# Two-layer encoder on one core: where the memory keys are transposed, how the memory values are split, and when some sums are made in the first chunks

## The chip, the core and the metric

One NeuronCore of a Trainium2 chip runs the whole kernel as one program. The metric is the device time of one execution in microseconds (us); the median of several runs counts. In the profiled execution the granted clock of TensorE was 1.00 throughout.

## The reference, cut to what matters

Two encoder layers on 512 tokens of width 1024, all in float32. Layer 0 mixes tokens with dilated window attention, layer 1 with grouped-query attention; both also attend, with 4 heads of 128, into 256 memory tokens:

```python
def memory_attention(q_mem, mem_h, w_kv, qn_g, kn_g):
    q = rmsnorm(q_mem.reshape(Bn, S, MEM_HEADS, HEAD_DIM), qn_g) * (HEAD_DIM ** -0.5)
    kv = jnp.einsum('bnd,de->bne', mem_h, w_kv).reshape(Bn, N, 2, MEM_HEADS, HEAD_DIM)
    k = rmsnorm(kv[:, :, 0], kn_g)
    v = kv[:, :, 1]
    s = jnp.einsum('bqhe,bkhe->bhqk', q, k).astype(jnp.float32)
    p = jax.nn.softmax(s, axis=-1).astype(v.dtype)
    return jnp.einsum('bhqk,bkhe->bqhe', p, v).reshape(Bn, S, MEM_W)
```

Each layer norms its input, projects it with one wide weight matrix, gates the heads' outputs and projects back: `x = x + jnp.einsum('bse,ed->bsd', y, w_out[i])`. The change concerns the first stretch of layer 0: the memory keys and values, and the first projections of x.

## The kernel before, in words

**Precision by halves.** Every float32 factor is split into a rounded part and a remainder. ScalarE (ACT) casts a weight tile to `wh` (L313), VectorE (DVE) subtracts to get `wo` (L323), and TensorE (PE) multiplies activation high by weight high (L175), activation low by weight high (L176) and activation high by weight low (L179). Four `wh` and four `wo` buffers form a ring.

**Seven products.** A projection of x is made by a scheme with seven products of half-size quarters instead of eight (`s_chunk`). The activations' combinations are called 12, 11, S1, S2, S4, S3, 22 in the order of the products; the weights' are "21", "11", T1, T2, "22", T3, T4. T1 is made by a DVE addition of two loaded pieces (L282), T2 by a DMA issued from GpSimd (POOL) that adds T1 onto another piece (L287), T3 by such a DMA from the weights in DRAM (L292), T4 by one that adds T2 onto "21" (L297). Bank by bank, ACT keeps a snapshot `sn` of a product (L388) and DVE adds the next ones to it (L405, L399). S2 and S4 come from DVE sums (L577, L579) behind S1 and S3 (L565, L566); each combination is then split by an ACT cast (L163, L573) and a DVE subtraction (L166, L574).

**What sets the order.** The program of each engine is written out in a fixed order while a `Driver` counts slots. After each group of matmuls on PE (a group: one pair of weight tiles on one block, or one weight tile on all blocks) the driver's `tick` advances a slot and resumes the generators that are due: `yield n` in one of them means "go on n slots later". `drv.release` starts one after a bank is complete, `drv.late` and `drv.soon` put a function at the end of this slot or the start of the next. `Weights.advance` runs once per group: it splits at most two weight tiles, makes at most one weight sum (`sum`), casts up to two tiles (`hi`) and issues loads (`dma`). `ripe` says how many groups must have passed since a load was issued or a sum made: LEAD = 2 unless told otherwise.

**The first chunks**, in the order in which PE takes them: the memory keys (four groups), the memory values (four groups), then the first projection by seven products (14 groups of 2.72 us: the values of the first window group, `v0`), then the memory queries (7 groups), then the eight heads. In between, PE transposes: x into `xT` for the activations (`turn4`, L505), and the normed memory keys into `qT` (`transpose4`, L610). Both use the four PSUM buffers of tag `at`. A group's result stands in one of four buffers `pj`.

**The memory keys and values** (`mem_kv`). A block of 128 keys is normed (L598, L453, L603), transposed two slots later (L610), and written as `kmT` by ACT (L647) and, LO_K[0] = 9 slots later, its remainder by DVE (L650). A block of values is scaled by ACT from PSUM to `vm` (L675) and its remainder made by DVE from the same PSUM bank (L678) at once, so the bank is held until DVE has read it. `kmT` and `vm` are read by the memory attention, whose first scores stand behind the first head's third product.

**Buffers.** 23 SBUF buffers of tag `m4` (128 x 1024) hold weight pieces, x, the key and value tiles and more. A load takes a free one when the program is written, and waits on the chip for the last reader of what was in it.

Of the kernel before, what the change touches and what calls it, by code (L numbers as in the profile page):

```python
# [10 lines left out]
F32 = mybir.dt.float32  # L11
F32R = mybir.dt.float32r
AF = mybir.ActivationFunctionType
ALU = mybir.AluOpType
# [11 lines left out]
MEM_STEP = 1, 1  # L26
MEM_D = 4
DIRECT, DIRECT_B = (7,), (4, 5, 6, 7)
LO_K, LO_V = (9, 5), (0, 3)
PD = 2  # L30
EO = 2, 2, 1, 2, 2, 1
YB = {"m": (2, 2), "k": (1, 1, 1), 0: (1, 2, 1), 1: (1, 2, 1)}
# [10 lines left out]
KEEP_C = {0: 14, 3: 14, 4: 12}  # L43
# [87 lines left out]
def trunk_kernel(ctx: ExitStack, tc: tile.TileContext, x, mem, wall, norm_g, mem_norm_g, gcol,  # L131
                 qn_a, kn_a, qn_b, kn_b, ident_d, mask_d, tab_a, tab_b, out):
    nc = tc.nc
    V, A, G, T = nc.vector, nc.scalar, nc.gpsimd, nc.tensor
# [11 lines left out]
    def m4(dt=F32, name="m4"):  # L146
        return pool.tile([128, 1024], dt, tag="m4", name=name, bufs=NM4)
# [47 lines left out]
    class Weights:  # L195
# [71 lines left out]
        def sum(self, force=False, want=None):  # L267

            for n, (key, d) in enumerate(self.sums[:8]):
                if want and key != want:  # L270
                    continue
                c, k, x = key
                if not c and not force and self.g < SUM_AT.get(k, 0):
                    break
                if k == "T1" and c >= T1_DMA:
                    if not self.ripe(self.load_at, key, force):
                        continue
                    G.dma_start(self.tile[key], wall[d], accum_op=ALU.add)
                elif k == "T1":
                    if not (self.ripe(self.load_at, key, force) and self.ripe(self.at, (c, "11", x), force)):  # L280
                        continue
                    V.tensor_tensor(self.tile[key], self.tile[key], self.tile[c, "11", x], ALU.add)  # L282
                    self.use((c, "11", x))
                elif k == "T2":
                    if not (self.ripe(self.load_at, key, force) and self.ripe(self.at, (c, "T1", x), force, 1 if c < T1_DMA else None)):
                        continue
                    G.dma_start(self.tile[key], self.tile[c, "T1", x], accum_op=ALU.add)  # L287
                    self.use((c, "T1", x))
                elif k == "T3":
                    if not self.ripe(self.load_at, key, force):  # L290
                        continue
                    G.dma_start(self.tile[key], wall[d], accum_op=ALU.add)  # L292
                else:
                    if not (self.ripe(self.lo_at, (c, "21", x), force, 1) and self.ripe(self.at, (c, "T2", x), force, T4_AT.get(c))):
                        continue
                    self.tile[key] = self.tile[c, "21", x]
                    G.dma_start(self.tile[key], self.tile[c, "T2", x], accum_op=ALU.add)  # L297
                    self.use((c, "T2", x))
                self.at[key] = self.g
                self.sums.pop(n)  # L300
                return True
            return False
# [161 lines left out]
    rm = pool.tile([128, 6], F32, name="rm")  # L464
# [188 lines left out]
    def mem_kv(layer, M, mid=None):  # L653
        kt_ = [m4(F32R, "kmT").rearrange("p (h t) -> p h t", h=4) for _ in range(2)]
        vt_ = [m4(F32R, "vm").rearrange("p (b e) -> p b e", b=2) for _ in range(2)]

        def ev_k(b, p):
            r = head_sq(p) if layer else head_sq(p, by=rm[:, 2 + b:3 + b])

            def rest():  # L660
                if not layer:
                    G.tensor_scalar(r, r, rm[:, b:b + 1], None, ALU.mult)
                xn = head_mul(p, r)
                yield 2
                q = transpose4(xn)
                cs = slice(b * 128, (b + 1) * 128)
                yield from put_norm(q, gk_m[layer], kt_[0][:, :, cs], kt_[1][:, :, cs], LO_K[layer])

            drv.release(rest(), 2)
            yield 1  # L670

        def ev_v(b, p):

            h = 0.5 if layer else rm[:, 4 + b:5 + b]
            A.activation(vt_[0][:, b], p, AF.Copy, scale=h)  # L675
            if b and LO_V[layer]:
                yield LO_V[layer]
            V.scalar_tensor_tensor(vt_[1][:, b], p, h, vt_[0][:, b].bitcast(F32), ALU.mult, ALU.subtract)  # L678
            yield 1

        proj_t(M, NAT[:2], ev_k, mid)
        proj_t(M, NAT[:2], ev_v)
        return kt_, vt_

# [276 lines left out]
    def prep():  # L961

        n = {}
        for c in range(5):
            if c < 4:
                n[c] = norm_1(xb[c], c == 2)
            if c:
                norm_2(xb[c - 1], n[c - 1], rows["x"])
            if 1 < c < 4:
                first_t(H, xb[c - 2], c - 2)  # L970
            yield 1

        def forms(c):
            yield from diffs_t(H, xb[2 + c], c)
            yield 2
            yield from rest_t(H, c, (2, 2, 2))

        drv.spawn(forms(1), 1)
        yield from forms(0)
# [57 lines left out]
    p = turn4(mg[0, 0], None, None)  # L1037
# [631 lines left out]
```

## Time and profile before

| What | Value |
|---|---|
| Median of 3 runs | 953.63 us (952.09 to 953.82) |
| The profiled execution | 953.29 us, its span 951.4 us |
| PE busy | 937.2 us of the span (99%) |
| VectorE (DVE) busy | 790.0 us (83%) |
| ScalarE (ACT) busy | 681.1 us (72%) |
| GpSimd (POOL) busy | 340.0 us (36%) |
| PE's idle time in the first 100 us that it spent waiting for DVE | 3.6 us in three waits (2.3, 0.9, 0.4) |

A row of a timeline gives start, duration, engine, line of the kernel, operation, output<-input, shape and count, and in brackets how long the engine had been idle before and what ended that. Rows of instructions that follow each other on one engine overlap a little (one DVE operation of 128 x 1024 shows 1.22 us, and the next starts 1.13 us after it), so distances are taken from start to start. The 1.9 us between the span and the time of the profiled execution lie around the span and belong to every run.

### The profile page before, as it was taken

How to read it: one execution, taken by the hardware profiler on the slowest of the kernel's cores; microseconds unless marked ns; L12 is line 12 of the kernel's file. 1: busy time of each engine (PE TensorE's matmuls, PEld its weight loads, DVE VectorE, ACT ScalarE, POOL GpSimd, SP SyncE). 2: the span in 40 equal slices, each digit the busy share in tenths (PEclk: the TensorE clock that was granted, in tenths of full speed). 3: DMA queues.
4: the chain of work that ended last, by engine and by line, in shares of the span. 5: the costliest groups of instructions: out<-in, count | busy, mean ns of one | idle time of the engine just before them, and what ended most of it. 6: DMA issues, size and time to landing. Idle time of an engine off the chain costs nothing.

```text
span 951.4 us, 16573 instructions
## 1 busy us (share of the span) xinstructions
PE 937.2 (99%) x5680; PEld 830.7 (87%) x5680; DVE 790.0 (83%) x1411; ACT 681.1 (72%) x1698; POOL 340.0 (36%) x484
## 2 busy tenths in 40 slices
PE   8999999999999999999999999999899999999998
PEld 6789888888888888888889998888899999998886
DVE  6997676878888888889798999868978998769982
ACT  7775689676868686868676768457778886878860
POOL 3323323656554545464827011213233241011110
PEclk9999999999999999999999999999999999999999
DMA  9999946869787878696868989979876686776524
GB/s 352 387 252 326 283 97 160 298 118 273 153 254 148 258 154 265 156 266 133 254 169 194 275 202 247 283 275 297 227 166 140 179 237 174 213 201 177 127 57 127
DMA packets 86198, 203.51 MB, mean 214 GB/s; under 512 B 25057, under 2 KB 34529, under 8 KB 86114
## 3 DMA queue, kind: packets, MB, share of 16 engines
q1 hardware_dynamic: 66962, 139.46, 42.9%
q0 software_dynamic: 17856, 60.83, 34.3%
q10 hardware_dynamic: 1296, 2.16, 0.6%
q8 instruction: 45, 0.74, 0.3%
q14 instruction: 39, 0.32, 0.1%
HBM read 156.48 MB, written 11.34 MB: 176 GB/s over the span
## 4 chain that ended last, share of the span: by engine, by line
PE 90%; DVE 4%; ACT 2%; DMA 2%; issue 1%; POOL 0%; SPq 0%; DVEq 0%; ACTq 0%; POOLq 0%
PE pj L176 24%; PE pj L175 24%; PE pj L179 24%; PE qT L610 2%; PE sa L1189 2%; PE oo L1297 2%; PE pt L1276 1%; PE ptb L1499 1%; DVE wo L323 1%; PE sa L1185 1%; PE ob L179 1%; DMA odb<-o 1%; PE pmt L735 1%; DMA m<-in_mem_dram 1%; PE ob L176 1%
## 5 line engine op out<-in xcount | busy, mean ns | idle before, releaser
L323 DVE TENSOR_TENSOR wo<-wl,wh 128x1024 fp32r<-128x1024 f32 x255 | 315.0, 1241 | 6.3 <-ACT wh L313 5.9
L313 ACT CAST wh<-wl 128x1024 fp32r<-128x1024 f32 x255 | 268.8, 1060 | 32.9 <-PE pj L176 19.2
L175 PE MATMUL pj<-wh,hS 128*128 128x512 f32 (+1 forms) x448 | 157.4, 365 | 1.7 <-DVE sn L405 1.7
L176 PE MATMUL pj<-wh,hS 128*128 128x512 f32 (+1 forms) x448 | 152.2, 353 | 0.6 <-DVE hS L574 0.6
L175 PE MATMUL pj<-wh,h 128*128 128x512 f32 (+1 forms) x336 | 117.8, 364 | 0.0
L176 PE MATMUL pj<-wh,h 128*128 128x512 f32 (+1 forms) x336 | 114.1, 353 | 1.1 <-DVE h L574 1.1
L453 POOL TENSOR_TENSOR rstd<-mse,half 128x4 f32<-128x4 f32 (+2 forms) x96 | 101.4, 1056 | 8.0
L179 PE MATMUL pj<-wo,hS 128*128 128x512 f32 (+1 forms) x448 | 99.9, 352 | 0.0
L175 PEld LDWEIGHTS pj<-wh,hS 128*128 128x128 f32 x448 | 84.8, 189 | 12.1 <-DVE sn L405 2.1
L176 PEld LDWEIGHTS pj<-wh,hS 128*128 128x128 f32 x448 | 84.9, 190 | 11.0 <-DVE hS L574 0.8
L179 PEld LDWEIGHTS pj<-wo,hS 128*128 128x128 f32 x448 | 74.7, 189 | 11.8
L452 POOL TENSOR_SCALAR mse<-hss 128x4 f32<-128x4 f32 (+1 forms) x86 | 42.6, 495 | 112.9 <-ACT junk L598 108.5
L388 ACT COPY sn<-pj 128x512 f32<-128x512 f32 x116 | 64.5, 590 | 24.0 <-PE pj L179 23.2
L1133 POOL TENSOR_TENSOR ta<-sn,tabs 128x128 f32<-128x128 f32 (+1 forms) x64 | 39.8, 629 | 116.6 <-DVE sn L603 91.1
L598 ACT ACTIVATE junk<-sn 128x128 f32<-128x128 f32 x264 | 79.2, 309 | 1.2 <-DVE sn L399 1.2
L179 PE MATMUL pj<-wo,h 128*128 128x512 f32 (+1 forms) x336 | 74.8, 352 | 0.0
L176 PEld LDWEIGHTS pj<-wh,h 128*128 128x128 f32 x336 | 63.7, 190 | 8.8 <-DVE h L574 1.3
L175 PEld LDWEIGHTS pj<-wh,h 128*128 128x128 f32 x336 | 63.6, 189 | 7.3
L405 DVE TENSOR_TENSOR sn<-pj,sn 128x512 f32<-128x512 f32 x87 | 59.6, 686 | 8.5 <-PE pj L179 8.1
L297 POOL DMA_DIRECT2D wl<-wl x33 | 29.5, 903 | 103.7 <-DVE wo L323 54.5
L179 PEld LDWEIGHTS pj<-wo,h 128*128 128x128 f32 x336 | 56.0, 189 | 8.8
L287 POOL DMA_DIRECT2D wl<-wl x33 | 31.3, 976 | 72.7 <-DVE wl L282 21.4
(252 smaller groups left out, 2363.6 us busy)
## 6 DMA issues: line engine op xcount, KB each, us to landing
wl<-in_wall_dram SPq DMA_DIRECT2D x222, 512.0 KB, 7.4
wl<-wl POOLq DMA_DIRECT2D x66, 512.0 KB, 6.2
wl<-in_wall_dram POOLq DMA_DIRECT2D x42, 512.0 KB, 8.6
od<-o SPq DMA_DIRECT2D x11, 256.0 KB, 5.7
og<-od SPq DMA_DIRECT2D x10, 256.0 KB, 9.4
x<-in_x_dram SPq DMA_DIRECT2D x4, 512.0 KB, 9.0
v0d<-sn SPq DMA_DIRECT2D x8, 256.0 KB, 8.4
acc<-in_x_dram POOLq DMA_DIRECT2D x8, 256.0 KB, 6.4
```

What stands on the lines that cost most here:

```text
L175: T.matmul(o, a, b, start=start, stop=False, skip_group_check=True)
L176: T.matmul(o, c, d, start=False, stop=False, skip_group_check=True)
L179: T.matmul(o, a, b, start=False, stop=stop, skip_group_check=True)
L287: G.dma_start(self.tile[key], self.tile[c, "T1", x], accum_op=ALU.add)
L313: A.copy(wh, self.tile[self.items[i]])
L323: V.tensor_tensor(wo, self.tile[key], wh.bitcast(F32), ALU.subtract)
L388: A.copy(t, b)
L405: V.tensor_tensor(t, b, t, ALU.subtract if q == "12" else ALU.add)
L452: G.tensor_scalar(e, ss, EPS, None, ALU.add)
L453: G.tensor_tensor(r, e, half[:, 0:n], ALU.pow)
L598: A.activation(jk, p[:, j * 128:(j + 1) * 128], AF.Square, scale=by, accum_out=ss[:, j:j + 1])
L1133: G.tensor_tensor(ta[:, 0:n], xn[:, 0:n, 0:32], ropeA[:, 0, b, s0:s0 + n], ALU.mult)
```

## The change

Four edits; all act on layer 0's first chunks alone (for layer 1 the old numbers and the old way of making the values stay).

- **Keys transposed later.** The wait ahead of the transposes `qT` goes from 2 to 8 slots (`TURN_K[0]`), and that of the remainder behind them from 9 to 4 (`LO_K[0]`).
- **Values split from a copy.** ACT first copies the scaled bank to a new SBUF tile `vr` (L682), one slot later casts it to `vm` (L684), and DVE makes the remainder nine slots after that from `vr` and `vm`, both in SBUF (L686). There is one more `m4` buffer in use, and two more ACT instructions.
- **S2 and S4 later.** `forms` waits 3 slots instead of 2 before the sums for the fourth and fifth product.
- **T1 later.** For the chunks named in KEEP_C (the first projection, the memory queries and the first head) the DVE addition for T1 must wait four groups after its load is issued instead of two.

```diff
-LO_K, LO_V = (9, 5), (0, 3)
+LO_K, TURN_K, LO_V = (4, 5), (8, 2), (9, 3)
...
-                    if not (self.ripe(self.load_at, key, force) and self.ripe(self.at, (c, "11", x), force)):
+                    if not (self.ripe(self.load_at, key, force, 4 if c in KEEP_C else None) and self.ripe(self.at, (c, "11", x), force)):
...
+        raw = None if layer else m4(name="vr")
...
-                yield 2
+                yield TURN_K[layer]
...
-            h = 0.5 if layer else rm[:, 4 + b:5 + b]
-            A.activation(vt_[0][:, b], p, AF.Copy, scale=h)
-            if b and LO_V[layer]:
+            if layer:
+                A.activation(vt_[0][:, b], p, AF.Copy, scale=0.5)
+                if b:
+                    yield LO_V[layer]
+                V.scalar_tensor_tensor(vt_[1][:, b], p, 0.5, vt_[0][:, b].bitcast(F32), ALU.mult, ALU.subtract)
+            else:
+                t = raw[:, b * 512:b * 512 + 512]
+                A.activation(t, p, AF.Copy, scale=rm[:, 4 + b:5 + b])
+                yield 1
+                A.copy(vt_[0][:, b], t)
                 yield LO_V[layer]
-            V.scalar_tensor_tensor(vt_[1][:, b], p, h, vt_[0][:, b].bitcast(F32), ALU.mult, ALU.subtract)
+                V.tensor_tensor(vt_[1][:, b], t, vt_[0][:, b].bitcast(F32), ALU.subtract)
...
         def forms(c):
             yield from diffs_t(H, xb[2 + c], c)
-            yield 2
+            yield 3
             yield from rest_t(H, c, (2, 2, 2))
```

Up to the memory values, and from the first head on, each engine's instructions stand in the same order as before; the line numbers behind the edits are higher by 8. In between, three places matter. The first is VectorE's program from the second half of the normed x (L499) to the S1 of both token halves (`hS`), before:

```order
L499 SCALAR_TENSOR_TENSOR x<-x,rstd,row 128x512 x2
L323 TENSOR_TENSOR wo<-wl,wh 128x1024 x2
L678 SCALAR_TENSOR_TENSOR vm<-pj,rm,vm 128x512
L282 TENSOR_TENSOR wl<-wl 128x1024
L565 TENSOR_TENSOR fS_515<-xT,f_476 128x512
L566 TENSOR_TENSOR fS_516<-f_369,xT 128x512
L166 TENSOR_TENSOR hS_519<-fS_515,hS_519 128x4x128
L678 SCALAR_TENSOR_TENSOR vm<-pj,rm,vm 128x512
```

and with the change:

```order
L499 SCALAR_TENSOR_TENSOR x<-x,rstd,row 128x512 x2
L323 TENSOR_TENSOR wo<-wl,wh 128x1024 x2
L282 TENSOR_TENSOR wl<-wl 128x1024
L565 TENSOR_TENSOR fS_509<-xT,f_477 128x512
L566 TENSOR_TENSOR fS_510<-f_370,xT 128x512
L166 TENSOR_TENSOR hS_513<-fS_509,hS_513 128x4x128
L323 TENSOR_TENSOR wo<-wl,wh 128x1024 x2
```

Both remainders of the values have left this place; they stand some 30 instructions later. On PE, the transposes `xT` and `qT` ahead of the first projection's first groups (`h` is the split x), before, where a line of dots stands for the L175 and L176 rows of a group:

```order
L505 MATMUL xT<-ident,x 128x128 x8
L610 MATMUL qT<-ident,xn 128x128 x4
...
L179 MATMUL pj<-wo,act 128x512 x4
L610 MATMUL qT<-ident,xn 128x128 x4
L505 MATMUL xT<-ident,x 128x128 x8
...
L179 MATMUL pj<-wo,h_351 128x512 x4
```

and with the change, where the two `qT` stand behind the fifth and sixth group of the projection (S1, `hS`):

```order
L505 MATMUL xT<-ident,x 128x128 x8
...
L179 MATMUL pj<-wo,act 128x512 x4
L505 MATMUL xT<-ident,x 128x128 x8
...
L179 MATMUL pj<-wo,hS_513 128x512 x4
L610 MATMUL qT<-ident,xn 128x128 x4
...
L179 MATMUL pj<-wo,hS_513 128x512 x4
L610 MATMUL qT<-ident,xn 128x128 x4
```

PE has two transposes fewer ahead of the first projection, and two `at` buffers fewer are taken there. The third place is VectorE again, from the setup of the rotary tables (`grA`) to the snapshots of the memory queries, before:

```order
L992 TENSOR_SCALAR grA<-grA 128x96
L405 TENSOR_TENSOR sn<-pj,sn 128x512
L323 TENSOR_TENSOR wo<-wl,wh 128x1024 x2
L282 TENSOR_TENSOR wl<-wl 128x1024
L323 TENSOR_TENSOR wo<-wl,wh 128x1024
L399 TENSOR_TENSOR sn<-sn 128x512 x2
L405 TENSOR_TENSOR sn<-pj,sn 128x512
L323 TENSOR_TENSOR wo<-wl,wh 128x1024
L282 TENSOR_TENSOR wl<-wl 128x1024
```

and with the change:

```order
L1000 TENSOR_SCALAR grA<-grA 128x96
L686 TENSOR_TENSOR vm<-vr,vm 128x512
L405 TENSOR_TENSOR sn<-pj,sn 128x512
L323 TENSOR_TENSOR wo<-wl,wh 128x1024 x3
L399 TENSOR_TENSOR sn<-sn 128x512 x2
L405 TENSOR_TENSOR sn<-pj,sn 128x512
L323 TENSOR_TENSOR wo<-wl,wh 128x1024
L282 TENSOR_TENSOR wl<-wl 128x1024
```

The first of the two T1 additions of the first head (L282) now stands behind a third split, the two L399 and an L405, and one of the values' remainders stands right behind the setup. On ACT, the two casts L684 stand around the cast of the first T1 tile, and the casts of the first T2 tile and of S2's second half have changed places.

## The prediction

> **What bounds the kernel now.** I read the page first, then PE's waits in the first 100 us, then the timelines of PE, DVE, ACT and POOL around the two larger waits. The page:
>
> ```profile
> span 951.4 us, 16573 instructions
> PE 937.2 (99%) x5680; PEld 830.7 (87%) x5680; DVE 790.0 (83%) x1411; ACT 681.1 (72%) x1698; POOL 340.0 (36%) x484
> ```
>
> PE is the bound, so only a gap on PE is worth time, and an instruction moved along PE's program is worth none. PE's waits on DVE in the stretch that the change touches (us in total, times, longest):
>
> ```profile
> PE xT L505 <- DVE fS L566: 2.3, 1, 2.3
> PE pj L175 <- DVE sn L405: 0.9, 1, 0.9
> ```
>
> **The first gap, from PE's timeline:**
>
> ```profile
> 31.43 1.07 PE L179 MATMUL pj<-wo,act 128*128 128x512 f32 x4
> 32.35 1.03 PE L505 MATMUL xT<-ident,x 128*128 128x128 f32 x8
> 33.22 0.60 PE L610 MATMUL qT<-ident,xn 128*128 128x128 f32 x4
> 33.57 0.48 PE L175 MATMUL pj<-wh,act 128*128 128x512 f32 x1
> 35.51 1.08 PE L179 MATMUL pj<-wo,act 128*128 128x512 f32 x4
> 36.43 0.60 PE L610 MATMUL qT<-ident,xn 128*128 128x128 f32 x4
> 36.87 0.60 PE L505 MATMUL xT<-ident,x 128*128 128x128 f32 x4
> 39.78 0.63 PE L505 MATMUL xT<-ident,x 128*128 128x128 f32 x4 [2.32 <-DVE fS L566]
> 42.08 1.07 PE L179 MATMUL pj<-wo,h 128*128 128x512 f32 x4
> ```
>
> Between the L179 of 31.43 and that of 35.51 lie eight xT, four qT and one group: 4.08 us. From there to 42.08 the same work took 6.57, so the gap costs 6.57 - 4.08 = **2.49 us**. What was waited for is a PSUM buffer `at`: four transposed tiles in a row (two xT, two qT) fill all four, and the last xT needs the one that DVE's L566 reads. DVE's timeline says why that read is late:
>
> ```profile
> 34.29 2.35 DVE L323 TENSOR_TENSOR wo<-wl,wh 128x1024 fp32r<-128x1024 f32 x2
> 36.56 0.74 DVE L678 SCALAR_TENSOR_TENSOR vm<-pj,rm,vm 128x512 fp32r<-128x512 f32 x1
> 37.23 1.22 DVE L282 TENSOR_TENSOR wl<-wl 128x1024 f32<-128x1024 f32 x1
> 38.36 0.68 DVE L565 TENSOR_TENSOR fS<-xT,f 128x512 f32<-128x512 f32 x1
> 38.96 0.68 DVE L566 TENSOR_TENSOR fS<-f,xT 128x512 f32<-128x512 f32 x1
> 41.38 0.75 DVE L678 SCALAR_TENSOR_TENSOR vm<-pj,rm,vm 128x512 fp32r<-128x512 f32 x1 [0.97 <-ACT vm L675]
> ```
>
> **The second gap**, in the memory queries:
>
> ```profile
> 83.14 1.12 PE L179 MATMUL pj<-wo,h 128*128 128x256 f32 x8
> 86.02 1.12 PE L179 MATMUL pj<-wo,hS 128*128 128x256 f32 x8
> 88.08 0.38 PE L175 MATMUL pj<-wh,hS 128*128 128x256 f32 x1 [0.94 <-DVE sn L405]
> 90.09 1.12 PE L179 MATMUL pj<-wo,hS 128*128 128x256 f32 x8
> ```
>
> A group takes 86.02 - 83.14 = 2.88 us there and this one 4.07, so this gap costs **1.19 us**. DVE was late because it had stood still at a T1 addition whose load hadn't landed:
>
> ```profile
> 70.00 0.68 DVE L405 TENSOR_TENSOR sn<-pj,sn 128x512 f32<-128x512 f32 x1
> 70.60 5.34 DVE L323 TENSOR_TENSOR wo<-wl,wh 128x1024 fp32r<-128x1024 f32 x2
> 79.25 1.23 DVE L282 TENSOR_TENSOR wl<-wl 128x1024 f32<-128x1024 f32 x1 [3.31 <-DMA wl<-in_wall_dram]
> 87.34 0.69 DVE L405 TENSOR_TENSOR sn<-pj,sn 128x512 f32<-128x512 f32 x1
> ```
>
> **The change, part by part.**
>
> *Keys transposed later.* The eight transposes cost the same wherever they stand, about 0.4 us per four (36.87 - 36.43). Nobody needs them soon: `kmT` is read behind the first head's third product, which comes after the last row above. What counts is that two fewer `at` buffers are taken: the second pair of xT finds the two that the x of an earlier group had used. So the first gap goes, whatever DVE does: 2.49 us. The work uncovered next, the first projection's first group, needs nothing late: its weights were split in the row of 34.29.
>
> *Values from a copy.* L678 leaves DVE at 36.56 and 41.38 and takes its wait of 0.97 along. In its place come on ACT two casts L684, on DVE two L686 that read SBUF alone. Neither is in the trace; the nearest rows, of the same shape out of SBUF, are:
>
> ```profile
> L574 DVE TENSOR_TENSOR hS<-f,hS 128x512 fp32r<-128x512 f32 x4 | 2.8, 690 | 0.0
> L573 ACT CAST hS<-f 128x512 fp32r<-128x512 f32 x4 | 2.5, 618 | 1.0 <-DVE f L577 1.0
> 46.17 0.62 ACT L163 CAST hS<-fS 128x512 fp32r<-128x512 f32 x1 [4.82 <-DVE fS L565]
> ```
>
> I take 0.62 us per L684 and 0.69 per L686; bounds 0.5 to 1.05 and 0.6 to 2.5 (half and double the next larger shape). ACT pays 1.24 us in a place where it idles 4.82, but the S1 that ends this idling comes earlier now, so the casts stand ahead of the first T1 tile's cast and delay it. Following ACT and DVE row by row from 36.56 with the distances of the rows, DVE is ahead by 0.67 at L282 and by 0.67 + 0.97 + 0.67 = 2.3 at the second half of S1, then waits for ACT about 0.9 (T1's cast) and 0.4 (S2's cast). At its L405 of 70.00 it has the same work behind it as before: 70.0 - 0.97 - 0.12 (two L686 for two L678) + 1.3 = 70.1 to 70.2. **So DVE isn't faster in sum, while PE is 2.49 us earlier.** The cover for that is the wo of the fourth product's first tile:
>
> ```profile
> 55.47 1.22 DVE L323 TENSOR_TENSOR wo<-wl,wh 128x1024 fp32r<-128x1024 f32 x1
> 58.40 1.07 PE L179 MATMUL pj<-wo,hS 128*128 128x512 f32 x4
> ```
>
> It ended 1.7 us before PE asked for it. Its end moves from 56.69 to about 55.0 (2.3 won, 0.6 more because an L574 now stands behind it, 1.3 of new waits), PE's request to 58.40 - 2.49 = 55.9: 0.9 us of cover are left. If it is gone, each further 1 us on ACT or DVE costs 1 us.
>
> *S2 and S4 a slot later.* Nothing is added; this lets the wo of the first T1 tile go ahead of these sums, and it is in the 55.0 above. Cost 0.
>
> *T1 later.* The first head's two L282 move behind work that can go on. From L405 (70.00) to L405 (87.34) DVE took 17.34 us, of which 3.31 waiting; the same instructions in the new order, without a wait, take 14.03. So it starts at 70.15 + 14.03 = 84.2 and frees PE at 84.9 (it ends 0.05 before PE's 88.08 now). PE itself would be there at 88.08 - 1.19 - 2.49 = 84.4. PE therefore still waits 0.5 us, and is 88.08 - 84.9 = **3.2 us** ahead, of 3.68 possible. The new place of the first L282 is at about 80.1; there it has to find its load landed, as it does if the landing stays at 79.2.
>
> *One more buffer.* The `vr` tile moves each load of this stretch to another buffer with another last reader; the load of the first head's T1 must now wait for a T4 sum. From the DMA issues of the two windows:
>
> ```profile
> 48.38 1.05 POOL L297 DMA_DIRECT2D wl<-wl  x1
> wl<-wl POOLq DMA_DIRECT2D x1, 512.0 KB, 12.3
> 62.47 4.21 SPq L262 DMA_DIRECT2D wl<-in_wall_dram  x5
> wl<-in_wall_dram SPq DMA_DIRECT2D x1, 512.0 KB, 13.7
> ```
>
> That sum is issued at 48.38 and lands by 60.7; the load is one of the last of the five rows from 62.47 on and landed 13.7 us later. It was not held by this buffer and won't be: cost 0.
>
> **The sum.** Behind the memory queries all engines have the old order, and in the long rest PE is as full as can be, so 3.2 us reach the end:
>
> ```profile
> 150.00:950.00 800.00, 793.94 (x4914) 709.04 (x4912) 672.42 (x1258) 574.14 (x1456) 290.34 (x410) 1.00 0.77 203
> ```
>
> The profiled execution took 953.29 us, 1.9 more than its span; it becomes 953.29 - 3.2 = 950.1. The median shown, 953.63, is 0.34 above this execution, so as a median I forecast **950.4 us**.
>
> **A rule against the change.** In the row of 70.60 two splits took 5.34 us in place of 2.35. Beside them POOL ran the rotary tables, which start when DVE has done `grA`:
>
> ```profile
> 70.17 4.69 POOL L995 TENSOR_TENSOR tabs<-tabA,grA 128x768 f32<-128x768 f32 x2 [4.82 <-DVE grA L992]
> ```
>
> The Trainium skill, SBUF — State Buffer, "Who interferes with whom", says that a DVE instruction with two SBUF inputs contends with a GpSimd instruction that reads SBUF, that whoever starts first holds the port to its end, and that a DVE instruction with one SBUF input doesn't contend. By that rule the two rows agree (L405, which reads PSUM, took its normal 0.68 beside L995, and L323 didn't), and making the remainder from a copy, right behind `grA`, puts a third instruction into the way of L995.
>
> **The rivals.**
>
> 1. *The collision with POOL grows.* L686 starts with L995 and loses a whole one of its two (4.69 / 2 = 2.35 us), and the first L323 waits out the second. Before, 5.34 - 2.35 = 3.0 us were lost; then it is up to 4.1. For it: the two rows; against it: the same 4.69 us of POOL are to be waited out in both orders, and L686 may start first. DVE's chain to PE is 1.1 us later: 951.5.
>
> 2. *The first gain is given back at the fourth product.* ACT now casts the first T2 tile ahead of S2's second half, so a T2 sum that lands late stops both. It was issued by POOL (L287, behind the first L282) and landed 9.1 us later at 47.9; by my count it is wanted at 48.9:
>
> ```profile
> 38.77 1.08 POOL L287 DMA_DIRECT2D wl<-wl  x1 [6.44 <-DVE wl L282]
> wl<-wl POOLq DMA_DIRECT2D x1, 512.0 KB, 9.1
> ```
>
> If it took the 13.7 us of the load above, ACT would stand 2 to 3 us longer, the 0.9 us of cover would be gone, and DVE would bring the delay to the second gap: 3.2 - 2.1 = 1.1 gained, 952.5. Against it: L282 issues it 0.7 earlier.
>
> 3. *The other side: the T1 load of the first head lands later.* L282 at 80.1 waits for it with all of DVE behind it; each us of landing past 80.1 is one for PE. From a landing at 83.3 on nothing is won. If the other buffer puts its issue behind the next snapshots' transfers (to about 71.5), 13.7 us later is 85.2, hence 5.1 us lost against 3.2 won: 955.5. Against it: the gate opens at 60.7, before SP gets there.
>
> That the change doesn't do what it says is no rival here: the new order shows all four edits.
>
> **How the numbers follow.** Forecast 0.62; rival 1 0.14; rival 2 0.13; rival 3 0.07; the gain lost in some other way, around 953, 0.04. About 0.2% (1.9 us, to 951.7) is what a measurement of this kernel can tell from no change. Faster: 0.62 + 0.14 and a little of rival 2 = 0.78; same: 0.15; slower: 0.07. The range runs from 949.1 (all 3.68 us won, and the median 0.9 below as the runs spread) to 952.6 (rival 2), which leaves out rival 3 and the rest.
>
> **What would show it.** Right: no wait of xT on L566 near 37 us and about 2.5 us less up to the first projection; the L405 wait at 85 under 0.6 us; L282 near 80 with no wait on a load. Wrong: a wait of PE on a wo L323 or a snapshot between 50 and 60 (rival 2), over 3.5 us lost beside L995 (rival 1), an idle DVE ahead of L282 (rival 3). My weakest number is DVE's 70.1, which rests on two waits for ACT that I followed by hand.

## The result, and the profile after

The changed kernel takes **950.12 us** (median of 6 runs, 949.63 to 950.39) beside 953.46 for the kernel before on the same chip (6 runs, 952.09 to 954.32). The ratio is 0.9966, with a 95% interval of 0.9955 to 0.9977: 3.2 us faster. The profiled execution took 950.34 us with a span of 948.6, where before had 953.29 and 951.4. The head of the page of the changed kernel:

```profile
span 948.6 us, 16572 instructions
PE 938.2 (99%) x5680; PEld 831.8 (88%) x5680; DVE 789.7 (83%) x1411; ACT 680.8 (72%) x1700; POOL 339.0 (36%) x484
```

The shares tell nothing, as every engine has the same work to within about 1 us. PE's waits on DVE in the first 100 us do, in the same view as before (total, times, longest): the wait of xT on L566 is gone, that on L405 fell from 0.9 to 0.2, and the third, of 0.4 in the opening, doesn't appear.

```profile
PE pj L175 <- DVE sn L405: 0.2, 1, 0.2
```

**The first gap.** PE's timeline, from the last-but-one group of the memory values on:

```profile
31.85 1.07 PE L179 MATMUL pj<-wo,act 128*128 128x512 f32 x4
32.76 1.03 PE L505 MATMUL xT<-ident,x 128*128 128x128 f32 x8
...
35.46 1.07 PE L179 MATMUL pj<-wo,act 128*128 128x512 f32 x4
36.38 1.03 PE L505 MATMUL xT<-ident,x 128*128 128x128 f32 x8
...
39.08 1.07 PE L179 MATMUL pj<-wo,h 128*128 128x512 f32 x4
...
49.95 1.07 PE L179 MATMUL pj<-wo,hS 128*128 128x512 f32 x4
50.87 0.60 PE L610 MATMUL qT<-ident,xn 128*128 128x128 f32 x4
...
53.16 1.09 PE L179 MATMUL pj<-wo,hS 128*128 128x512 f32 x4
54.08 0.60 PE L610 MATMUL qT<-ident,xn 128*128 128x128 f32 x4
...
56.36 1.07 PE L179 MATMUL pj<-wo,hS 128*128 128x512 f32 x4
```

From 31.85 to 39.08 PE needs 7.23 us, before it needed 42.08 - 31.43 = 10.65. Of the difference of 3.42, 0.98 come back where the eight qT now stand (53.16 - 49.95 = 3.21 and as much for the next, each 0.49 above a group's 2.72). That leaves 2.44 for the wait, forecast at 2.49.

**DVE and ACT behind it.** DVE's timeline shows the two new waits on ACT, and the split that gives the fourth product's first wo:

```profile
36.98 1.23 DVE L282 TENSOR_TENSOR wl<-wl 128x1024 f32<-128x1024 f32 x1
...
38.72 0.68 DVE L566 TENSOR_TENSOR fS<-f,xT 128x512 f32<-128x512 f32 x1
...
46.36 1.23 DVE L323 TENSOR_TENSOR wo<-wl,wh 128x1024 fp32r<-128x1024 f32 x1 [0.78 <-ACT wh L313]
...
49.31 0.69 DVE L574 TENSOR_TENSOR hS<-f,hS 128x512 fp32r<-128x512 f32 x1 [0.39 <-ACT hS L573]
...
54.23 1.22 DVE L323 TENSOR_TENSOR wo<-wl,wh 128x1024 fp32r<-128x1024 f32 x1
```

ACT's timeline shows the two new casts L684, and ahead of the snapshots L388 and the T2 cast of 49.17 no wait at all:

```profile
44.76 0.62 ACT L684 CAST vm<-vr 128x512 fp32r<-128x512 f32 x1
45.28 1.04 ACT L313 CAST wh<-wl 128x1024 fp32r<-128x1024 f32 x1
46.23 0.61 ACT L684 CAST vm<-vr 128x512 fp32r<-128x512 f32 x1
46.75 1.06 ACT L388 COPY sn<-pj 128x512 f32<-128x512 f32 x2
...
49.17 1.06 ACT L313 CAST wh<-wl 128x1024 fp32r<-128x1024 f32 x1
```

**The second gap.** DVE's timeline around the memory queries; the first head's first T1 addition stands at 80.53 and finds its load there:

```profile
70.22 0.69 DVE L686 TENSOR_TENSOR vm<-vr,vm 128x512 fp32r<-128x512 f32 x1
70.83 0.69 DVE L405 TENSOR_TENSOR sn<-pj,sn 128x512 f32<-128x512 f32 x1
71.43 6.25 DVE L323 TENSOR_TENSOR wo<-wl,wh 128x1024 fp32r<-128x1024 f32 x3
...
80.53 1.21 DVE L282 TENSOR_TENSOR wl<-wl 128x1024 f32<-128x1024 f32 x1
...
84.54 0.68 DVE L405 TENSOR_TENSOR sn<-pj,sn 128x512 f32<-128x512 f32 x1
```

And PE's timeline there:

```profile
83.98 1.12 PE L179 MATMUL pj<-wo,hS 128*128 128x256 f32 x8
85.27 0.39 PE L175 MATMUL pj<-wh,hS 128*128 128x256 f32 x1 [0.17 <-DVE sn L405]
87.29 1.12 PE L179 MATMUL pj<-wo,hS 128*128 128x256 f32 x8
```

The group at the second gap takes 87.29 - 83.98 = 3.31 us, 0.43 above the 2.88 of its neighbours; before, it was 1.19 above.

### The profile page after: what moved, and what is told of

Read it like the earlier page. It is cut to its first block, busy times and chain, and to the rows that moved or that the text cites. A ratio compares the mean times of both kernels' runs of the same rounds, so it can differ in the third digit from the quotient of the medians.

```text
span 948.6 us, 16572 instructions
## 1 busy us (share of the span) xinstructions
PE 938.2 (99%) x5680; PEld 831.8 (88%) x5680; DVE 789.7 (83%) x1411; ACT 680.8 (72%) x1700; POOL 339.0 (36%) x484
## 4 chain that ended last, share of the span: by engine, by line
PE 85%; DVE 7%; DMA 3%; ACT 2%; issue 1%; POOL 0%; SPq 0%; DVEq 0%; ACTq 0%; POOLq 0%
PE pj L176 22%; PE pj L175 22%; PE pj L179 22%; DVE wo L323 3%; PE qT L610 2%; DMA og<-od 1%; PE ptb L1507 1%; PE sa L1197 1%; PE oo L1305 1%; PE pt L1284 1%; DMA wl<-in_wall_dram 1%; PE sa L1193 1%; PE xT L505 1%; PE ob L179 1%; PE ob L176 1%
## 5 line engine op out<-in xcount | busy, mean ns | idle before, releaser
L175 PE MATMUL pj<-wh,hS 128*128 128x512 f32 (+1 forms) x448 | 157.6, 365 | 0.9 <-DVE sn L405 0.9
L176 PE MATMUL pj<-wh,hS 128*128 128x512 f32 (+1 forms) x448 | 152.3, 353 | 0.6 <-DVE hS L574 0.6
L175 PE MATMUL pj<-wh,h 128*128 128x512 f32 (+1 forms) x336 | 117.8, 364 | 0.0
L176 PE MATMUL pj<-wh,h 128*128 128x512 f32 (+1 forms) x336 | 114.2, 353 | 1.1 <-DVE h L574 1.1
L179 PE MATMUL pj<-wo,hS 128*128 128x512 f32 (+1 forms) x448 | 99.9, 352 | 0.0
L175 PEld LDWEIGHTS pj<-wh,hS 128*128 128x128 f32 x448 | 84.9, 189 | 11.2 <-DVE sn L405 1.4
L176 PEld LDWEIGHTS pj<-wh,hS 128*128 128x128 f32 x448 | 85.0, 190 | 11.0 <-DVE hS L574 0.8
L179 PEld LDWEIGHTS pj<-wo,hS 128*128 128x128 f32 x448 | 74.7, 189 | 11.8
L1141 POOL TENSOR_TENSOR ta<-sn,tabs 128x128 f32<-128x128 f32 (+1 forms) x64 | 37.6, 595 | 117.7 <-DVE sn L603 91.1
L388 ACT COPY sn<-pj 128x512 f32<-128x512 f32 x116 | 64.5, 590 | 20.9 <-PE pj L179 20.0
L179 PE MATMUL pj<-wo,h 128*128 128x512 f32 (+1 forms) x336 | 74.9, 352 | 0.0
L176 PEld LDWEIGHTS pj<-wh,h 128*128 128x128 f32 x336 | 63.7, 190 | 8.8 <-DVE h L574 1.3
L175 PEld LDWEIGHTS pj<-wh,h 128*128 128x128 f32 x336 | 63.7, 189 | 7.3
L405 DVE TENSOR_TENSOR sn<-pj,sn 128x512 f32<-128x512 f32 x87 | 59.6, 685 | 8.5 <-PE pj L179 8.1
L179 PEld LDWEIGHTS pj<-wo,h 128*128 128x128 f32 x336 | 56.1, 189 | 8.8
```

The source lines that it names most:

```text
L175: T.matmul(o, a, b, start=start, stop=False, skip_group_check=True)
L176: T.matmul(o, c, d, start=False, stop=False, skip_group_check=True)
L179: T.matmul(o, a, b, start=False, stop=stop, skip_group_check=True)
L388: A.copy(t, b)
L405: V.tensor_tensor(t, b, t, ALU.subtract if q == "12" else ALU.add)
L1141: G.tensor_tensor(ta[:, 0:n], xn[:, 0:n, 0:32], ropeA[:, 0, b, s0:s0 + n], ALU.mult)
```

## The experiments

The small effects lie between two places that can be found in every trace. **t6** is the start of the L179 row of the last-but-one group of the memory values (31.43 before, 31.85 after). **t28** is that of the last group of the memory queries (99.17 and 96.36). The stretch t28 - t6 leaves out what the opening did in an execution: t6 itself lay anywhere between 31.43 and 33.35, with one program order up to there. Each row of the table is one profiled execution. Behind t28 all kernels took 851.4 to 853.4 us, with no trend, so the 2.0 us by which this rest varies are as large as most effects here, and the ratios of many runs (last column) have to be read beside the stretch. In most rows the stretch shrank by more than the ratio says, by up to 1.4 us; the one execution of the kernel before, from which all differences are taken, may lie high. The column "landing" is when DVE's first L282 of the first head began, for the kernels in which it waited for its load.

| kernel | t6 | landing | t28 | t28 - t6 | against before | ratio, 95% interval |
|---|---|---|---|---|---|---|
| before | 31.43 | 79.25 | 99.17 | 67.74 | - | - |
| the change | 31.85 | - | 96.36 | 64.51 | -3.23 | 0.9966 [0.9955, 0.9977] |
| k1: keys later, alone | 31.95 | 78.99 | 98.90 | 66.95 | -0.79 | 0.9995 [0.9986, 1.0003] |
| k2: T1 later, alone | 31.61 | - | 98.17 | 66.56 | -1.18 | 0.9991 [0.9982, 0.9999] |
| k3: keys and T1 later | 31.74 | - | 97.16 | 65.42 | -2.32 | 0.9981 [0.9972, 0.999] |
| k4: the change, T1 as before | 33.35 | 79.43 | 99.34 | 65.99 | -1.75 | 0.9989 [0.998, 0.9998] |
| k5: the change, S2 and S4 as before | 31.79 | - | 95.87 | 64.08 | -3.66 | 0.9974 [0.9963, 0.9985] |
| k6: the change, values as before | 31.93 | - | 96.23 | 64.30 | -3.44 | 0.9972 [0.9964, 0.9981] |
| k7: the change, rotary tables on DVE | 31.76 | - | 97.47 | 65.71 | -2.03 | 0.9974 [0.9965, 0.9983] |
| k8: the change, one L686 three times | 32.36 | - | 98.51 | 66.15 | -1.59 | 0.9998 [0.9988, 1.0007] |
| k9: the change, keys as before | 31.79 | - | 97.69 | 65.90 | -1.84 | 0.9981 [0.9972, 0.999] |
| k10: values and S2, S4 alone | 31.74 | 77.66 | 97.74 | 66.00 | -1.74 | 0.9984 [0.9976, 0.9993] |
| k11: values from a copy, alone | 31.84 | 78.14 | 98.04 | 66.20 | -1.54 | 0.9986 [0.9978, 0.9995] |
| k12: S2 and S4 later, alone | 31.86 | 79.55 | 99.46 | 67.60 | -0.14 | 0.9998 [0.9989, 1.0007] |

The theory, once both traces were there, followed from the prediction's count of DVE ("DVE isn't faster in sum"): PE's early gap is worth nothing by itself, since DVE stands at the first head's T1 addition until the load lands, and holds PE in the memory queries. The rival was that the parts add up, each gap by its own size.

### k1, k2, k3 and k4: the two large parts apart

Keys later alone (k1) is the kernel before with these two edits:

```diff
-LO_K, LO_V = (9, 5), (0, 3)
+LO_K, TURN_K, LO_V = (4, 5), (8, 2), (0, 3)
...
-                yield 2
+                yield TURN_K[layer]
```

> The kernel before with the later key transposes alone (8 and 4 slots); values, S2/S4 and T1 as before. Theory (DVE's idle time at the first head's T1 addition, until its load lands near 79, sets when PE gets past the memory queries): the wait of xT on L566 near 37 us goes, 2.5 us, but PE then waits for the snapshot sum L405 about 1.2 + 2.5 = 3.7 us, and the time stays within 0.5 us of the kernel before. Rival (the two waits are independent): 2.5 us faster, the L405 wait still 0.9 to 1.2.

T1 later alone (k2) is the kernel before with this one; k3 has both:

```diff
-                    if not (self.ripe(self.load_at, key, force) and self.ripe(self.at, (c, "11", x), force)):
+                    if not (self.ripe(self.load_at, key, force, 4 if c in KEEP_C else None) and self.ripe(self.at, (c, "11", x), force)):
```

> The kernel before with the later T1 additions alone. Theory: DVE no longer stands 3.3 us in front of L282, so the L405 wait of 1.2 us goes; the wait of xT on L566 stays 2.3; 1.2 us faster, near 0.9987 of before. Rival (independent waits, or the landing just moves the wait): no faster, a wait of DVE of over 1 us at L282 in its new place.

> The kernel before with both the later key transposes and the later T1 additions; values still split from PSUM, S2/S4 as before. Theory (these two edits are the whole gain): both waits go but for a rest; 2.7 to 3.3 us faster, as the whole change. Rival (the copy is needed, since the remainders from PSUM keep DVE late): a wait of PE on a weight split or snapshot sum of 1 us or more in the fourth product near 55, and under 2 us faster.

k4 is the changed kernel without that edit:

> The changed kernel with the T1 additions back at two groups. Theory: DVE stands in front of the first head's L282 until the load lands near 79, and nearly the whole gain of 3.3 us is lost: within 0.6 us of the kernel before, the L405 wait of PE 3 us or more. Rival (independent waits): only 0.8 to 1.2 us of the gain is lost, the time near 951.2.

Keys later alone measured 0.9995, with an interval that holds 1: no time that a measurement can tell. The early gap was gone (its groups took 3.6 us each), and yet DVE waited at its L282 as before:

```profile
78.99 1.22 DVE L282 TENSOR_TENSOR wl<-wl 128x1024 f32<-128x1024 f32 x1 [3.12 <-DMA wl<-in_wall_dram]
```

PE gave most of the gain back in two places of k1, and not in one with a wait of 3.7 as I had expected. One of them was new:

```profile
49.24 0.50 PE L175 MATMUL pj<-wh,hS 128*128 128x512 f32 x1 [0.83 <-ACT sn L388]
...
87.81 0.39 PE L175 MATMUL pj<-wh,hS 128*128 128x256 f32 x1 [1.41 <-DVE sn L405]
```

The 0.79 us that k1's trace keeps are the landing's: it came 47.04 us behind t6 (78.99 - 31.95), and 47.82 before.

T1 later alone gave 1.18 us in the trace, the whole second gap. Both together gave 2.32: 1.1 us more than T1 alone, and 0.9 less than the whole change. So the theory for k3, that these two edits are the whole gain, missed. Its rival had the size by the ratio (1.8 us, under the 2 it named) but not the place, which was the S1 product and not the fourth. Where that last microsecond stays, k3's PE and ACT show. The S1 product's first group waits for ACT's snapshots, which stand in ACT's queue behind a cast of S2 that waits for DVE:

```profile
49.23 0.50 PE L175 MATMUL pj<-wh,hS 128*128 128x512 f32 x1 [1.04 <-ACT sn L388]
```

```profile
48.07 0.62 ACT L573 CAST hS<-f 128x512 fp32r<-128x512 f32 x1 [0.41 <-DVE f L577]
48.60 1.07 ACT L388 COPY sn<-pj 128x512 f32<-128x512 f32 x2
```

In the changed kernel the same snapshots began at 46.75 and PE did not wait for them.

k4 missed what I had expected of it: the wait at L405 was 1.40 and not 3 or more, and the time lay below that of before. Its opening was 1.9 us late (t6 33.35), its load landed at 79.43, near that of before, and DVE stood there for only 1.52:

```profile
79.43 1.23 DVE L282 TENSOR_TENSOR wl<-wl 128x1024 f32<-128x1024 f32 x1 [1.52 <-DMA wl<-in_wall_dram]
```

So taking T1 back costs 65.99 - 64.51 = 1.5 us in the trace, with the landing the end of it again. In the three kernels that waited for it so far, t28 lay 19.92, 19.91 and 19.91 us behind the landing (before, k1, k4), while t28 - t6 differed by 1.75. That is the mark of a chain that begins at the landing (k10 below is the exception).

### k5 and k6: the two small parts, each taken back

The changed kernel with S2 and S4 where they were (k5), and with the values split from PSUM as before (k6, the old L675 to L678):

```diff
             yield from diffs_t(H, xb[2 + c], c)
-            yield 3
+            yield 2
```

> The changed kernel with the sums for S2 and S4 back at two slots; the copy of the values stays. Theory (the snapshots L388 only have to stand clear of S2's cast or to find it early; one of the two small edits is enough): PE starts the S1 product without a wait, since DVE, freed of L678, has the sum L577 ready by 46.2; 3.0 to 3.3 us faster than before, as the whole change. Rival (the order of the sums alone counts): a wait of PE on ACT's L388 of 1 us near 48, as with the two other edits alone, and 1.8 to 2.2 us faster.

> The changed kernel with the values' remainders made from PSUM at once, as before; the other three edits stay. Theory (one of the two small edits is enough): the two L388 stand ahead of S2's cast, the wait of PE on them is under 0.3 us, DVE is as late at its L405 near 70 as with the copy, and the time is 2.8 to 3.3 us below before. Rival (the copy is needed for DVE): a wait of 1 us or more in the S1 product or in the fourth product, and about 2 us faster.

Neither costs anything: 64.08 and 64.30 against 64.51, and the ratios lie well within each other's intervals. In neither did PE wait for the snapshots; ACT began them at 47.20 in k5 and at 47.55 in k6, against 48.60 in k3, which has neither. Beside keys and T1 later, one of the two small edits is enough: either brings 1.1 to 1.3 us over k3 in the trace, the second one nothing more. By the ratios it is 0.7 to 0.9, but their intervals overlap with k3's, so this point rests on the traces: the wait of PE on L388 is there in k3 and in neither of these. k5 lacks the residual wait at L405 altogether and is 0.43 shorter than the change in the trace, but not by the ratio.

### k7 and k8: the collision with POOL

In k7 the rotary tables' two instructions L1003 run on DVE in place of POOL; in k8 the second remainder L686 is computed three times, with the same result each time. DVE's L686 and POOL's L1003 are L687 and L1004 in k8.

```diff
-            G.tensor_tensor(ropeA[:, cs_], tabA[:, cs_, :, None, :].to_broadcast([128, 4, 6, 32]),
+            V.tensor_tensor(ropeA[:, cs_], tabA[:, cs_, :, None, :].to_broadcast([128, 4, 6, 32]),
```

> The changed kernel with the two multiplications of the rotary tables on DVE instead of POOL. Theory (POOL's reads slow the three splits beside them by 2.9 us, and DVE's chain still holds PE up by 0.4): the splits take 1.2 each, the tables about 0.9 each on DVE, DVE is 1.1 us earlier, the last wait of PE in the memory queries goes, and PE is through them 0.4 us earlier than in the changed kernel. Rival (the splits are slow for another reason, such as the loads): they stay slow, DVE is 1.8 us later and PE waits 2 us.

```diff
-                V.tensor_tensor(vt_[1][:, b], t, vt_[0][:, b].bitcast(F32), ALU.subtract)
+                for _ in range(3 if b else 1):
+                    V.tensor_tensor(vt_[1][:, b], t, vt_[0][:, b].bitcast(F32), ALU.subtract)
```

> The changed kernel with the second remainder of the values made three times instead of once, 1.2 us more on DVE behind the setup of the tables; the result is the same. Theory (DVE's chain up to the snapshot sum sets when PE gets past the memory queries, microsecond for microsecond): PE waits 1.6 us instead of 0.4 there, and the time is 1.2 us above the changed kernel. Rival (that chain has slack, or it is the landing that counts): under 0.5 us more.

On k7's DVE, with POOL silent, each split takes its normal 1.22 us and each table 0.95. But a wait came in that no other kernel had, for a table that the setup multiplies, and with it the kernel is no faster than the change (0.9974):

```profile
72.23 0.21 DVE L1000 TENSOR_SCALAR grA<-grA 128x96 f32<-128x96 f32 x1 [2.28 <-DMA grA<-in_qn_a_dram]
...
73.56 1.22 DVE L323 TENSOR_TENSOR wo<-wl,wh 128x1024 fp32r<-128x1024 f32 x1
74.69 0.95 DVE L1003 TENSOR_TENSOR tabs<-tabA,grA 128x768 f32<-128x768 f32 x1
```

So k7 shows who slows the splits, and leaves open what the tables' place is worth in time. k8's DVE, and its POOL beside it:

```profile
70.57 5.26 DVE L687 TENSOR_TENSOR vm<-vr,vm 128x512 fp32r<-128x512 f32 x3
75.75 0.68 DVE L405 TENSOR_TENSOR sn<-pj,sn 128x512 f32<-128x512 f32 x1
76.35 3.48 DVE L323 TENSOR_TENSOR wo<-wl,wh 128x1024 fp32r<-128x1024 f32 x3
```

```profile
70.74 4.54 POOL L1004 TENSOR_TENSOR tabs<-tabA,grA 128x768 f32<-128x768 f32 x2 [6.27 <-DVE grA L1001]
```

Now the remainders carry the collision, 5.26 us for three in place of 0.69 for one, and the three splits behind POOL's end take their normal 3.48. The loss doesn't add up, it moves to whichever two-input instructions stand beside the tables. It cost 66.15 - 64.51 = 1.64 us in the trace, beside the 1.2 expected. The place was another one: PE waited for a weight split in the last group of the first projection, and for L405 it lost only 0.25 (its group took 3.13):

```profile
77.62 1.20 PE L179 MATMUL pj<-wo,h 128*128 128x512 f32 x4 [1.54 <-DVE wo L323]
```

By the ratios it cost about 3 us. The table's column from one trace lies outside the interval of the ratio here, and by a little for k5, and inside or at its edge for all others. Part of the difference goes with the clock: in four of k8's twelve runs the mean granted clock was 0.996 to 0.998, and these took 954.2 to 955.1 us. The other eight have a median of 952.4, 1.4 to 1.9 above k5, k6 and k7 beside it (950.5 to 950.9), which is about what the trace shows. Why the clock was lower in those four stays open.

### k9: the change with the keys as before

```diff
-LO_K, TURN_K, LO_V = (4, 5), (8, 2), (9, 3)
+LO_K, TURN_K, LO_V = (9, 5), (2, 2), (9, 3)
```

> The changed kernel with the keys transposed where they stood before. Theory (DVE's work sets PE's pace once T1 is late, and an early gap costs only what the later one doesn't give back): the xT wait on L566 is back, at about 1.8 us, since no L678 stands ahead of L566 any more; in exchange the residual wait of 0.43 at L405 goes. So the memory queries end 1.8 - 0.43 = 1.4 us later than in the changed kernel by the seventh group (65.9 from it), the time is 1.4 above the changed kernel's and 1.8 below the kernel before (ratio 0.9981). Rival A (as the turn alone is worth nothing, undoing it costs nothing): 64.5 from the seventh group, ratio 0.9966. Rival B (the gap is back in full, 2.49): ratio 0.9988, the first gap over 2.3.

Measured: 0.9981, and 65.90 from t6 to t28, as the theory had it. That the ratio agrees to the last digit is luck, as its interval is 0.0009 to either side. Rival A falls by the interval, and rival B by the gap: it is back at the smaller size, and no wait at L405 is left. PE's waits on DVE in k9:

```profile
PE xT L505 <- DVE fS L566: 1.7, 1, 1.7
```

Turning the keys alone gave 0.79 us in the trace and nothing clear in the ratio; it is worth 65.90 - 64.51 = 1.4 us in the trace once DVE no longer stands still behind it.

### k10, k11 and k12: what the small edits do alone

k10 is k9 with the T1 additions as before too; k11 and k12 have one of its two small edits each.

> The changed kernel with the keys and the T1 additions where they stood before, so only the copy of the values and S2 and S4 a slot later are left. Theory (the first head's T1 load lands at about 79.2 us whatever PE and DVE did ahead of it, and DVE stands at that addition): L282 waits for its load until 78.9 to 79.5, the last memory-query group starts at 98.9 to 99.4, time within 0.4 us of the kernel before (ratio 0.9996 to 1.0004). Rival (the two small edits are worth their 1 us by themselves): last memory-query group at about 98.2, time 0.9 to 1.1 below, ratio 0.999.

Here the theory fell in two points. The time was 0.9984, 1.5 us faster, and not within 0.4 of before. DVE's wait shows the first:

```profile
77.66 1.23 DVE L282 TENSOR_TENSOR wl<-wl 128x1024 f32<-128x1024 f32 x1 [1.35 <-DMA wl<-in_wall_dram]
```

The landing isn't fixed, it came 1.6 us earlier. And it no longer sets t28: the group for which PE waited before takes 2.89 us, as much as its neighbours, and PE has no wait for L405 at all.

```profile
85.78 1.12 PE L179 MATMUL pj<-wo,hS 128*128 128x256 f32 x8
88.67 1.12 PE L179 MATMUL pj<-wo,hS 128*128 128x256 f32 x8
```

So 97.74 - 77.66 = 20.08 has some slack in it, and k10's 1.74 us are the whole second gap (1.19) and 0.55 of the first, which shrank from 6.57 to 6.02 with L678 gone ahead of L566. k9 tells the same from the other side: it is k10 with T1 later, and 0.10 us shorter (65.90 beside 66.00), so T1 later is worth next to nothing while PE is late from the first gap and the load lands early enough that PE needn't wait for DVE. The two single edits were to say which of them moves the landing.

> The kernel before with nothing but the values split from an SBUF copy. In the run with both small edits the first head's T1 load landed at 77.66 us, 1.6 earlier than before, and DVE stood only 1.35 us at its addition. Theory (with the copy DVE is earlier by its L678 while it adds and splits weights near 40 us, so buffers come free and loads are issued earlier): the landing is at 77.4 to 77.9, the last memory-query group starts 19.9 to 20.1 behind it at about 97.7, time 1.2 to 1.6 us below before, ratio 0.9984. Rival (S2 and S4 a slot later did it): landing at 79 and later, last memory-query group at 99, ratio 0.9997.

> The kernel before with nothing but S2 and S4 a slot later. Theory (the copy moves the landing, this doesn't): L282 waits for its load until about 79, the last memory-query group starts 19.9 later at 98.9 to 99.2, the first gap stays at 2.49, time within 0.4 us of before, ratio 0.9997. Rival (this edit moves the landing): landing at about 77.7, last memory-query group at 97.7, ratio 0.9984.

It is the copy: 0.9986 for k11, 0.9998 for k12, and a landing at 78.14 beside 79.55 with the same t6 to 0.02 (a little later than the 77.4 to 77.9 that I had expected). DVE's second T1 addition of the first projection and the first of the first head in k11, where no L678 stands ahead of them:

```profile
42.34 1.22 DVE L282 TENSOR_TENSOR wl<-wl 128x1024 f32<-128x1024 f32 x1
...
78.14 1.23 DVE L282 TENSOR_TENSOR wl<-wl 128x1024 f32<-128x1024 f32 x1 [2.44 <-DMA wl<-in_wall_dram]
```

and in k12, where L678 and its wait of 0.97 for ACT do stand there:

```profile
41.82 0.75 DVE L678 SCALAR_TENSOR_TENSOR vm<-pj,rm,vm 128x512 fp32r<-128x512 f32 x1 [0.97 <-ACT vm L675]
...
44.76 1.22 DVE L282 TENSOR_TENSOR wl<-wl 128x1024 f32<-128x1024 f32 x1
...
79.55 1.23 DVE L282 TENSOR_TENSOR wl<-wl 128x1024 f32<-128x1024 f32 x1 [2.83 <-DMA wl<-in_wall_dram]
```

The addition at 42.34 is 2.4 us earlier than that at 44.76, and the transfer that POOL issues behind it is as well. POOL's timeline in k11:

```profile
43.87 0.88 POOL L287 DMA_DIRECT2D wl<-wl  x1 [4.28 <-DVE wl L282]
```

and in k12:

```profile
46.28 0.88 POOL L287 DMA_DIRECT2D wl<-wl  x1 [5.99 <-DVE wl L282]
```

SP's next weight load goes out at 54.03 in k11 and at 56.95 in k12, and the first head's load lands 1.4 us earlier. Whether that is handed on by the earlier transfers or comes from the other buffers that the loads got through the `vr` tile wasn't separated. In both t28 follows the landing by 19.90 and 19.91 us. In all five kernels in which L405 then held PE up (before, k1, k4, k11, k12) the distance is 19.90 to 19.92, for landings from 78.14 to 79.55. k4's landing at 79.43 now reads in another way too: it is k10's 77.66 plus the 1.61 us by which k4's opening was later (79.27), so the landing seems to move with the opening. Counted from t6 it came at 45.9 to 46.3 us in the three kernels with the copy that waited for it (k4, k10, k11) and at 47.0 to 47.8 in the three without (before, k1, k12).

## Why the prediction was right

**The sum.** Forecast: 3.2 us less, 950.4. Measured: 0.9966 times 953.46 is 3.2 less, and 3.23 less from t6 to t28 in the trace. It held step by step where a step could be read: the wait of xT worth 2.49 (2.44), two new waits of DVE on ACT of 0.9 and 0.4 (0.78 and 0.39), L684 at 0.62 and L686 at 0.69 (0.62 and 0.69), L282 with no wait at about 80.1 (80.53 with an opening 0.42 later, so 80.11), the residual wait in the memory queries of 0.5 (0.43). DVE's L405, which I called my weakest number, was forecast for 70.1 to 70.2 and stood at 70.83, or 70.41 without the late opening. That this did no harm is luck: from there to the L405 that frees PE DVE took 84.54 - 70.83 = 13.71 us where I had 14.03, and the two errors of about 0.3 cancel.

**Rival 1, the collision with POOL.** It didn't grow. L686 began at 70.22, ahead of the tables, and took its normal 0.69; POOL's timeline has them at

```profile
70.39 5.06 POOL L1003 TENSOR_TENSOR tabs<-tabA,grA 128x768 f32<-128x768 f32 x2 [6.27 <-DVE grA L1000]
```

and the splits lost 6.25 - 3.48 = 2.8 us, against 3.0 before. The runs show who is slowed: remainders with two SBUF inputs in k8 (5.26 for three), the splits in the other kernels but not when POOL is silent (k7), and not L405, which reads PSUM and took its 0.69 beside the tables. The Trainium skill's rule (SBUF — State Buffer, "Who interferes with whom") agrees with these runs. That POOL stood behind L686 here, and not L686 behind POOL, shows in the first of POOL's two rows, which took 2.26 us where it had taken 1.87 before with L405 in L686's place; no run forced the order the other way round with the rest unchanged.

**Rival 2, the fourth product.** The T2 cast of 49.17 had no wait ahead of it, and DVE gave the wo of that product's first tile at 54.23 + 1.22 = 55.45. PE reached for it with the row of 56.36: 0.9 us of cover, as forecast.

**Rival 3, a later landing.** The addition at 80.53 found its load. The copy makes the load land earlier and not later (78.14 and 77.66, above). Whether that comes through the other buffers, which was the rival's mechanism, or through the earlier T1 addition is not shown.

**What the prediction had wrong, without harm to the sum.** First, "the work uncovered next, the first projection's first group, needs nothing late" looked one group ahead only. The group that comes late is the first of S1, for ACT's snapshots (k3, 1.04 of wait, 1.34 in the group). Second, the copy and the later S2 and S4 stand in the sum at a cost of 0 and a gain of 0. In truth they take away just that wait, each alone enough (k5, k6): without both, the gain in the trace is 2.3 and not 3.2 (k3). My row-by-row count of DVE and ACT had them in their new order, so their effect sat unseen in the times it gave. Third, "if the landing stays at 79.2" did not hold with the copy, which alone is worth 1.3 us by its ratio, through this landing. With T1 later as well, DVE no longer asks for that load before it is there, and the earlier landing buys nothing.

**Where the 3.2 us came from.** Not from parts that add up, though the four alone come near it in sum (0.79, 1.54, 1.18 and 0.14 us in the traces, together 3.65). By the ratios the keys later alone are worth nothing that can be measured, the copy alone 1.3, T1 later alone 0.9. Any two of these three parts, with S2 and S4 later as well: 1.0 to 2.7 (k4, k9, k6). What a part is worth depends on the others. In the traces T1 later is worth 1.18 alone, 1.5 as the last part (k4) and 0.10 beside the small edits (k9, k10); the copy 1.54 alone and nothing as the last part (k6). With the keys later and T1 early, PE's lead runs into a DVE that stands at the landing; with T1 later and the keys early, DVE's lead runs into a PE that is late from the first gap. Only where both go, and the snapshots are on time, does the whole of it reach the end.

## What to carry to other kernels

An early gap on the busiest engine is worth little while another engine stands behind it waiting for an event that the gap doesn't move: look for the next such wait downstream, and check with the distance from that event to a later place. It stays the same (19.90 to 19.92 us in five kernels here) while everything ahead of it moves, and a longer distance (20.08 in k10) says that the event no longer counts. A move that measured as nothing alone (k1) was worth 1.4 us in the trace as the last of several (k9), so a part is to be tried by taking it out of the whole as well as by putting it in alone. And where a wait goes, follow the engine past the next group to the next thing that it needs from each of the other engines.

## What the runs showed of the hardware

The loss beside POOL's tables hardly depends on what DVE does there. Two splits lost 5.34 - 2.35 = 3.0 us, three lost 2.8, and three remainders of half the size lost 3.4 (5.26, where three that start 0.6 apart, as L405 behind L686 at 70.22 and 70.83, take 1.9), for 4.5 to 5.1 us of POOL. Taken one by one, the rows of k8 show the two engines taking turns: L687 from 70.57 to 71.26, POOL's first table to 72.99, the second L687, which had started at 71.29, to 73.54, POOL's second to 75.28, the third L687 to 75.83. Each of POOL's two instructions holds up one of DVE's there, and no more than that.

The granted clock differs between kernels that do the same work. In 39 of the 106 runs of the kernel before that the experiments recorded, its mean was 0.997 or 0.998, and these took 954.0 us on average beside 953.1 for the other 67. k2, k8 and k12 had 10 such runs of 35, all other kernels, the changed one among them, none of 99. So a few tenths of a microsecond in the ratios can be clock and not order. No profiled execution had the lower clock, and what brings it about isn't shown.

A load of 48 KB can take microseconds longer to land with the same program up to there. The DMA issues between 50 and 76 us, with the median time to landing last, of k7:

```profile
grA<-in_qn_a_dram SPq DMA_DIRECT2D x1, 48.0 KB, 16.1
```

and of the changed kernel:

```profile
grA<-in_qn_a_dram SPq DMA_DIRECT2D x1, 48.0 KB, 10.7
```

The opening, in one program order, ended between 31.43 and 33.35 us (t6) in the 14 profiled executions, a spread of 1.9 us beside a change worth 3.2, so two traces are to be compared from a place behind it.
